# Inverse roots of a decoder layer started by one reciprocal-root activation instead of a logarithm and an exponential

## The chip, the cores and the metric

The kernel runs on one core of a Trainium2 chip. The metric is the device time of one execution in microseconds (us), as the median of several runs.

## The reference

One inference step of one decoder layer, for 256 prompt tokens and 8 decode tokens (264 columns, `T`) that share the weights; the width is 2048.

```
x = x + 1/2 * SwiGLU_1(RMSNorm(x))
h = RMSNorm(x); h @ w_in -> retention q/k/v/gate, attention q/k/v, indexer q/k/weights, two branch gates
A = retention(q, k, v), RMS-normed per head, * silu(gate)
B = top-k sparse attention, q and k RMS-normed per head
x = x + (sigmoid(g_A) * (A @ w_ret_out) + sigmoid(g_B) * (B @ w_att_out)) @ w_o
x = x + 1/2 * SwiGLU_2(RMSNorm(x))

def rms_norm(x, g):
    y = x * lax.rsqrt(mean(x * x, -1) + EPS)
    return y * g
```

Every RMS norm needs the inverse square root of a mean of squares.

## The kernel before

Activations lie transposed in SBUF: 128 features by 264 columns a block. Each weight block of 128 output features (`mblock`, L254 to L256 for its products) arrives in pieces of 128x1024 as 32-bit floats. ScalarE copies a piece to a rounded high part (`wh`, L248), VectorE or, for some pieces of the middle stage, GpSimd subtracts to get the low part (`wl`, L251), and TensorE adds up three products for each 128x128 block (high by high, high by low, low by high). Four buffers each of `wr`, `wh` and `wl` let the two splits run ahead, and three PSUM buffers (`ps`) let TensorE run up to three blocks ahead of whoever reads them.

The order of the work: the first FFN (weights `w1a`, `w2a`), then the middle stage (combined input projection, indexer, retention, attention, output projections), then the second FFN. In the middle stage the small tasks are generators in named queues; a weight block calls `step` with rates and so deals them out between weight products. A planner that estimates durations puts the instructions of each engine in order, with priorities (`ahead`), and in the middle stage only TensorE keeps the order of the program; ScalarE, VectorE, GpSimd and the DMA queues are ordered by the planner. At run time every engine works through its own list in order, so an instruction that waits holds up what stands behind it.

There are ten inverse roots, all by `root` (L262, L263) and `newton` (L266 to L268, VectorE). Three are for the norms of the model width (`Norm.done` through `rsqrt`, 128x264): at the start of the first FFN, of the middle stage and of the second FFN. Six go through `rms_roots` (128x528): two for the attention keys (`k_task`) and four for the retention heads (`group_norm`, which then scales `ro` at L1068). One is for the attention queries (`q_roots`, 128x33), whose result also scales rows that are written to DRAM and read back.

ScalarE evaluates a function only while a table that holds it is loaded; the program contains an ACT_TABLE_LOAD wherever the next function is not in the table loaded before. The other functions of ScalarE are Copy, Identity, Square, Relu, Silu (L325, L1192), Sigmoid (L1077) and the Exp of the two softmaxes (L768 for `psc` of the prompt, L858 for `sd` of decode).

Of the kernel before, what the change touches and what calls it, by code (L numbers as in the profile page):

```python
# [13 lines left out]
AF = mybir.ActivationFunctionType  # L14
# [108 lines left out]
def layer(ctx: ExitStack, tc: tile.TileContext, xT, gains, consts, dmat, didx, pt, state, cidx, ck, cv,  # L123
          w1a, w2a, wik, win, wro, wao, wo, w1b, w2b,
          yT, o_st, o_k, o_v, o_ik, o_sts):
    nc = tc.nc
# [26 lines left out]
    def wt(s="w", shape=(P, T), dt=F32, tag="w", bufs=8):  # L153
        return work.tile(list(shape), dt, tag=tag, name=nm(s), bufs=bufs)
# [104 lines left out]
        return ps[:m, :T]  # L259

    def root(ms, y, t):
        nc.scalar.activation(t, ms, AF.Ln)  # L262
        nc.scalar.activation(y, t, AF.Exp, scale=-0.5)  # L263

    def newton(y, ms, t):
        nc.vector.tensor_tensor(t, y, y, op=ALU.mult)  # L266
# [3 lines left out]
    def rsqrt(src, y, ms, t):  # L270

        nc.vector.tensor_scalar(ms, src, EPS, None, op0=ALU.add)
        root(ms, y, t)
        newton(y, ms, t)
# [393 lines left out]
    def rms_roots(sums):  # L668

        ss, y, t = (mt(n, (P, 2, T)) for n in ("ss", "y", "t"))  # L670
        for j, f in enumerate(sums):
            pq = aux()
            f(pq[:, :T])
            nc.scalar.activation(ss[:, j, :], pq[:, :T], AF.Identity, bias=epst)
        yield
        root(ss, y, t)
        yield
        newton(y, ss, t)
        yield y
# [468 lines left out]
    def q_roots():  # L1148
        qsq = mt("qsq", (P, NB, AH))
        nc.scalar.activation(qsq.rearrange("p b h -> p h b"), QS, AF.Square)  # L1150
        nc.vector.tensor_scalar(QS, QS, gqs, None, op0=ALU.mult)
        qrow = mt("qrow", (P, NB, AH))
        nc.vector.tensor_copy(qrow.rearrange("p b h -> p h b"), QS)
        yield
        pq = aux()
        nc.tensor.matmul(pq[:, :1], qsq.rearrange("p b h -> p (b h)"), ones128[:, :1], start=True, stop=True)
        pr = auxm()
        nc.tensor.transpose(pr[:, :P], qrow.rearrange("p b h -> p (b h)"), ident)
        qm, qt = st([P, 33], tag="qm", bufs=1), st([P, 33], tag="qt", bufs=1)
        qy = st([P, 33], tag="qy", bufs=1)  # L1160
        nc.vector.tensor_scalar(qm[:, 32:], pq[:, :1], EPS, None, op0=ALU.add)
        nc.vector.tensor_scalar(qm[:, :32], QSS.rearrange("p h t -> p (h t)"), EPS, None, op0=ALU.add)
        root(qm, qy, qt)
        newton(qy, qm, qt)
        nc.vector.tensor_copy(qsr, qy[:, 32:])
        nc.vector.tensor_copy(QR.rearrange("p h t -> p (h t)"), qy[:, :32])
        rt = mt("rt", (P, P))
        nc.scalar.activation(rt, pr[:, :P], AF.Copy, scale=qsr)
        nc.scalar.dma_start(rows[2], rt)
        yield  # L1170
# [46 lines left out]
    for m in range(KB):  # L1217
        ps = mblock(wao[m], 16, AHI, ALO)
        t = wt("at")
# [101 lines left out]
```

## Time and profile before

| | |
|---|---|
| median of 3 runs (lowest to highest) | 2666.53 us (2664.01 to 2667.66) |
| profiled execution, its own time | 2688.78 us |
| its span, first to last instruction | 2686.8 us |
| TensorE matmuls busy | 2614.1 us, 97% of the span |
| VectorE busy | 1534.2 us, 57% |
| ScalarE busy | 1172.4 us, 44% |
| GpSimd busy | 703.3 us, 26% |
| mean granted TensorE clock | 0.987 of full |

The times of single instructions below come from the profiled execution. It took 22 us more than the median of the runs, so a sum made of its rows is a difference to its own time and is carried to the median as a difference. In the rows PE is TensorE, DVE VectorE, ACT ScalarE, POOL GpSimd, SP the engine that issues DMAs; a q behind a name is the engine's instruction queue; xN merges N neighbouring instructions.

### The profile page before, as it was taken

What the parts mean: (1) busy time and instruction counts of PE and PEld (TensorE: products, weight loads), DVE (VectorE), ACT (ScalarE), POOL (GpSimd) and SP (SyncE); (2) the same over time, 40 slices, a digit from 0 to 9 for tenths busy, and PEclk for the clock granted to TensorE, in tenths of its full rate; (3) what the DMA queues carried; (4) which work ended last, traced back from release to release, by engine and by line L of the source; (5) the groups of instructions that cost most, each with busy time, mean ns of one, the idle gap of its engine ahead of it and who ended that gap; (6) DMA issues with size and microseconds to landing.
All of it is one profiled execution on the core that took longest, in us unless ns stands there. A gap on an engine that the chain in (4) does not pass through costs nothing.

```text
span 2686.8 us, 51545 instructions
## 1 busy us (share of the span) xinstructions
PE 2614.1 (97%) x21207; PEld 2586.1 (96%) x21207; DVE 1534.2 (57%) x2288; ACT 1172.4 (44%) x1559; POOL 703.3 (26%) x575
## 2 busy tenths in 40 slices
PE   7999999999999999999988899999999999999999
PEld 7999999999998899989888899999999999999999
DVE  6555555555564777534689745556655555554554
ACT  5443344334453434533546644444544334433443
POOL 3110011001265353245388353231111001100110
PEclk9999999999999999999999999999999999999999
DMA  6556555665575455456686566666577666765655
GB/s 217 181 181 181 181 182 181 183 183 183 170 240 181 138 179 171 128 181 218 219 290 219 182 202 226 207 217 201 182 238 231 210 189 224 240 207 181 216 165 174
DMA packets 173965, 529.09 MB, mean 197 GB/s; under 512 B 22705, under 2 KB 43761, under 8 KB 173729
## 3 DMA queue, kind: packets, MB, share of 16 engines
q1 hardware_dynamic: 148384, 488.31, 57.5%
q10 hardware_dynamic: 19440, 21.90, 2.4%
q0 software_dynamic: 5904, 15.59, 1.7%
q8 instruction: 166, 2.72, 0.4%
q14 instruction: 71, 0.57, 0.1%
HBM read 504.12 MB, written 21.60 MB: 196 GB/s over the span
## 4 chain that ended last, share of the span: by engine, by line
PE 87%; issue 3%; POOL 3%; DVE 2%; ACT 2%; DMA 2%; ACTq 0%; SPq 0%; POOLq 0%; DVEq 0%
PE ps L254 28%; PE ps L255 28%; PE ps L256 28%; POOL sb L958 1%; POOL wl L251 1%; POOL pr L836 1%; ACT wh L248 1%; DVE ro L1068 0%; DVE wl L251 0%; DVE psc L775 0%; DMA gs<-s 0%; DMA x<-xT 0%; PE aux L1038 0%; DMA qb<-rows 0%; DMA qq<-rows 0%
## 5 line engine op out<-in xcount | busy, mean ns | idle before, releaser
L248 ACT ACTIVATE wh<-wr 128x1024 fp32r<-128x1024 f32 x866 | 901.1, 1043 | 1339.3 <-PE ps L255 882.8
L251 DVE TENSOR_TENSOR wl<-wr,wh 128x1024 fp32r<-128x1024 f32 (+2 forms) x798 | 983.4, 1233 | 674.4 <-ACT wh L248 636.0
L254 PE MATMUL ps<-hi,wh 128*128 128x264 f32 x4624 | 1335.1, 289 | 20.3 <-ACT hi L287 10.2
L256 PE MATMUL ps<-hi,wl 128*128 128x264 f32 x4624 | 1321.6, 286 | 10.7 <-DVE wl L251 5.5
L255 PE MATMUL ps<-lo,wh 128*128 128x264 f32 x4624 | 1322.6, 286 | 5.1 <-issue 3.7
L254 PEld LDWEIGHTS ps<-hi,wh 128*128 128x128 f32 x4624 | 879.8, 190 | 29.6 <-issue 11.7
L256 PEld LDWEIGHTS ps<-hi,wl 128*128 128x128 f32 x4624 | 877.2, 190 | 14.6 <-DVE wl L251 7.0
L255 PEld LDWEIGHTS ps<-lo,wh 128*128 128x128 f32 x4624 | 879.2, 190 | 8.0 <-issue 5.3
L255 PE MATMUL ps<-hl,wh 128*128 128x264 f32 x1408 | 399.1, 284 | 0.4 <-issue 0.4
L256 PE MATMUL ps<-hh,wl 128*128 128x264 f32 x1408 | 398.9, 283 | 0.0
L254 PE MATMUL ps<-hh,wh 128*128 128x264 f32 x1408 | 398.8, 283 | 0.0
L327 POOL TENSOR_TENSOR s<-s,rstd 128x264 f32<-128x264 f32 x88 | 116.5, 1324 | 1012.1 <-ACT s L325 1012.1
L256 PEld LDWEIGHTS ps<-hh,wl 128*128 128x128 f32 x1408 | 264.4, 188 | 0.5 <-issue 0.5
L255 PEld LDWEIGHTS ps<-hl,wh 128*128 128x128 f32 x1408 | 264.7, 188 | 0.0
L254 PEld LDWEIGHTS ps<-hh,wh 128*128 128x128 f32 x1408 | 264.6, 188 | 0.0
L251 POOL TENSOR_TENSOR wl<-wr,wh 128x512 fp32r<-128x512 f32 x136 | 180.8, 1351 | 254.0 <-ACT wh L248 226.5
L836 POOL TENSOR_TENSOR pr<-qb,kb 128x512 f32<-128x512 f32 x64 | 102.3, 1629 | 22.4 <-issue 8.8
L988 POOL TENSOR_TENSOR kv<-ku,rvs 128x512 f32<-128x512 f32 x32 | 33.6, 1050 | 217.7 <-DMA ku<-rows 205.1
L990 DVE SCALAR_TENSOR_TENSOR su<-su,kv 128x256 f32<-128x256 f32 x64 | 24.4, 422 | 95.6 <-POOL kv L988 95.6
L359 POOL DMA_INDIRECT kt<-cidx,kix x64 | 72.8, 1138 | 18.1 <-issue 17.5
L334 DVE TENSOR_TENSOR h<-ps,s 128x264 f32<-128x264 f32 x88 | 38.1, 433 | 65.5 <-PE ps L256 61.5
L255 PE MATMUL ps<-alo,wh 128*128 128x264 f32 x256 | 72.9, 285 | 0.0
(317 smaller groups left out, 2310.8 us busy)
## 6 DMA issues: line engine op xcount, KB each, us to landing
wr<-win SPq DMA_DIRECT2D x224, 512.0 KB
wr<-w1a SPq DMA_DIRECT2D x176, 512.0 KB
wr<-w1b SPq DMA_DIRECT2D x176, 512.0 KB
wr<-w2a SPq DMA_DIRECT2D x80, 512.0 KB
wr<-w2b SPq DMA_DIRECT2D x80, 512.0 KB
wr<-wro SPq DMA_DIRECT2D x32, 512.0 KB
wr<-wao SPq DMA_DIRECT2D x32, 512.0 KB
wr<-wo SPq DMA_DIRECT2D x32, 512.0 KB
```

The source lines that it names most:

```text
L248: nc.scalar.activation(wh[:, :n, :m], wr[:, :n, :m], AF.Copy)
L251: eng.tensor_sub(wl[:, a:e, :m], wr[:, a:e, :m], wh[:, a:e, :m])
L254: nc.tensor.matmul(ps[:m, :T], wh[:, k, :m], hi[g], start=g == 0, stop=False)
L255: nc.tensor.matmul(ps[:m, :T], wh[:, k, :m], lo[g], start=False, stop=False)
L256: nc.tensor.matmul(ps[:m, :T], wl[:, k, :m], hi[g], start=False, stop=g == nk - 1)
L327: nc.gpsimd.tensor_mul(s2, s, rstd)
L334: nc.vector.tensor_mul(h, pu, s2)
L359: nc.gpsimd.indirect_dma_start(out=KT[p][pg // 8][:, o:o + PG], out_offset=None, in_=cidx, in_offset=bass.IndirectOffsetOnAxis(ap=kix[:, p ...
L836: nc.gpsimd.tensor_mul(pr[:, a:a + 1], qb[:, a:a + 1], k[:, a:a + 1].to_broadcast([P, 1, 4, P]))
L958: nc.gpsimd.tensor_mul(sb[:, a:a + 2], sb[:, a:a + 2], qq[:, a:a + 2, None, :].to_broadcast([P, 2, 2, P]))
L988: nc.gpsimd.tensor_mul(kv, k[:, :, None, :].to_broadcast([P, 2, 2, P]), v.to_broadcast([P, 2, 2, P]))
L990: nc.vector.scalar_tensor_tensor(s[:, i], s[:, i], g1[h + i], kv[:, i], op0=ALU.mult, op1=ALU.add)
```

## The change

The logarithm and the exponential of minus one half of it are replaced by one activation that gives the reciprocal of the root of the absolute value. The intermediate tile `t` is no longer written by ScalarE; it is still used by the Newton step, which stays.

```
     def root(ms, y, t):
-        nc.scalar.activation(t, ms, AF.Ln)
-        nc.scalar.activation(y, t, AF.Exp, scale=-0.5)
+        nc.scalar.activation(y, ms, AF.Abs_reciprocal_sqrt)
```

## Rows read from the trace of the kernel before

**Rows 1.** The page, busy time of each engine.

```profile
PE 2614.1 (97%) x21207; PEld 2586.1 (96%) x21207; DVE 1534.2 (57%) x2288; ACT 1172.4 (44%) x1559; POOL 703.3 (26%) x575
```

**Rows 2.** Windows by stage: stretch, its length, busy time (count) of each engine, PEclk, DMA.

```profile
40.00:796.00 756.00, 754.16 (x6226) 753.80 (x6225) 402.90 (x466) 318.58 (x390) 111.43 (x91) 1.00 0.61 186
...
1420.00:1540.00 120.00, 105.35 (x795) 101.28 (x793) 101.64 (x141) 80.69 (x139) 67.83 (x50) 0.96 0.60 195
...
1940.00:2680.00 740.00, 740.00 (x6096) 740.00 (x6095) 394.81 (x497) 298.29 (x344) 84.29 (x74) 1.00 0.66 208
```

**Rows 3.** Groups by line, ScalarE: shapes, count | busy us, mean ns | idle before.

```profile
L262 ACT ACT_TABLE_LOAD x10 | 12.8, 1283 | 0.3
L263 ACT ACT_TABLE_LOAD x10 | 12.8, 1283 | 0.2
...
L262 ACT ACTIVATE t<-ss 128x528 f32<-128x528 f32 x6 | 3.9, 646 | 0.1
...
L262 ACT ACTIVATE qt<-qm 128x33 f32<-128x33 f32 x1 | 0.2, 233 | 0.0
```

**Rows 4.** Timeline of ScalarE, first root: start, us, instruction [idle before <-what ended it].

```profile
36.71 0.42 ACT L262 ACTIVATE t<-ms 128x264 f32<-128x264 f32 x1
37.16 1.28 ACT L263 ACT_TABLE_LOAD   x1
38.45 0.42 ACT L263 ACTIVATE rstd<-t 128x264 f32<-128x264 f32 x1
```

**Rows 5.** Timeline of TensorE, the first wait behind that root.

```profile
44.44 0.36 PE L254 MATMUL ps<-hi,wh 128*128 128x264 f32 x1 [1.47 <-DVE h L334]
```

**Rows 6.** Timelines of VectorE and TensorE, first key root.

```profile
1112.35 0.71 DVE L266 TENSOR_TENSOR t<-y 128x528 f32<-128x528 f32 x1 [3.31 <-ACT y L263]
...
1113.72 0.15 DVE L589 TENSOR_SCALAR fill<-aux 128x1 f32<-128x1 f32 x1
```

```profile
1113.92 0.70 PE L1033 MATMUL aux<-rs,vr 128*128 128x256 f32 x2 [1.52 <-DVE fill L589]
```

**Rows 7.** Windows of low granted clock, columns as in rows 2.

```profile
1114.50:1121.30 6.80, 6.21 (x25) 5.54 (x24) 2.96 (x5) 0.77 (x2) 2.11 (x2) 0.50 0.39 117
...
1541.20:1548.00 6.80, 5.63 (x26) 5.63 (x27) 4.24 (x11) 4.62 (x8) 5.58 (x5) 0.50 0.83 298
```

**Rows 8.** Chain of waits behind the query root: start, us, what.

```profile
1293.55 1.84 DMA rows<-rt
...
1296.31 7.65 DMA qq<-rows
```

**Rows 9.** Timelines of VectorE and TensorE behind that read.

```profile
1306.67 1.22 DVE L953 TENSOR_REDUCE rd<-sb 128x8 f32<-128x1024 f32 x1 [3.93 <-POOL sb L958]
```

```profile
1319.22 0.51 PE L254 MATMUL ps<-hi,wh 128*128 128x264 f32 x1 [2.51 <-ACT wh L248]
1322.90 0.59 PE L256 MATMUL ps<-hi,wl 128*128 128x264 f32 x1 [2.96 <-DVE wl L251]
```

**Rows 10.** Timelines of ScalarE, VectorE and TensorE, second head root.

```profile
1469.87 1.28 ACT L1077 ACT_TABLE_LOAD   x1
```

```profile
1473.85 0.77 DVE L266 TENSOR_TENSOR t<-y 128x528 f32<-128x528 f32 x1 [1.41 <-ACT y L263]
```

```profile
1492.38 0.91 PE L1060 MATMUL aux<-sq,ones 128*128 128x264 f32 x3 [2.69 <-DVE psc L755]
```

**Rows 11.** Timeline of TensorE, third head root.

```profile
1514.27 0.49 PE L792 MATMUL aux<-pts,vn 128*128 128x128 f32 x2 [1.07 <-ACT pts L786]
```

**Rows 12.** Timelines of VectorE, ScalarE and TensorE, fourth head root.

```profile
1531.12 0.71 DVE L266 TENSOR_TENSOR t<-y 128x528 f32<-128x528 f32 x1 [5.07 <-ACT y L263]
```

```profile
1539.30 0.42 ACT L1192 ACTIVATE s<-g 128x264 f32<-128x264 f32 x1 [4.23 <-DVE g L1190]
1539.74 1.28 ACT L858 ACT_TABLE_LOAD   x1
```

```profile
1542.37 0.66 PE L869 MATMUL aux<-C,sd 128*128 128x128 f32 x2 [4.10 <-DVE sd L861]
```

## The prediction, written before the changed kernel had run

> **What bounds the kernel now.** I read the page first: matmuls fill 97% of the span and ScalarE, the engine that is changed, 44% [rows 1]. Work taken from ScalarE is worth nothing by itself; it counts only where TensorE stands still, or runs at its lower clock, because a root came late. The windows by stage say where that can be: between 40 and 796 us TensorE stands still for 1.8 us of 756, and between 1940 and 2680 us not at all, but between 1420 and 1540 us for 14.7 of 120 us, at a granted clock of 0.96 [rows 2]. So both FFNs are closed to a gain, except the first microseconds, and the middle stage is open. From there I went to the groups of ScalarE for the price of the edit [rows 3], then to the ten roots one by one in the timelines, asking of each which wait of TensorE ends behind it [rows 4 to 12].
>
> **What is removed.** Each of the ten roots is now a table load, a Ln, a second table load and an Exp: L262 and L263 have ten loads each of 1283 ns [rows 3]. Ln and Exp therefore do not share a loaded table here. The new root needs its table and one activation. I take 1283 ns for its load, since the loads of both functions cost that to the ns, and the Ln's own duration for its activation at each size (646, 425 and 233 ns; the middle one is the 0.42 us of rows 4): same tiles, same engine [rows 3, 4]. A price from zero up to that of the pair replaced would be the bounds; nothing that is added exceeds what is removed.
>
> How many loads go: one for each root, ten. Three more go between neighbours. Between the middle stage's norm and both key roots ScalarE runs only functions for which this trace shows no load (copies, squares, identities and relus), so the key roots find the table in place: two more loads. In the second head root a sigmoid with a load of its own stands between Ln and Exp [rows 10], so the table changes four times around it; with one activation it changes twice: one more besides the root's own. The count of the whole program should fall by 13. That is 13 x 1.283 = 16.7 us, and with the ten Exp of about 6 x 0.646 + 3 x 0.425 + 0.233 = 5.4 us ScalarE loses 22.1 us of its 1172.4.
>
> The Trainium skill, in "ScalarE: Activation LUTs", section "Table sets: the hidden batching unit", speaks against the change: it says that one set holds both Ln and Exp and that the pair costs one load. By that rule no load of a lone root would be saved, only the 0.42 to 0.65 us of one activation, and the sum below would shrink to about a third. This trace differs: a load stands ahead of each of the two, ten times, and so the rule gets no chance among the rivals. The same section says that the cheap functions are in every set; the absence of loads ahead of copies here agrees.
>
> **What of it lies on the path**, root by root in order of time. The shift of a root is the distance from the start of Ln to the start of Exp, since the one activation ends where Ln ended.
>
> First FFN: Ln begins at 36.71 and Exp at 38.45, so the root is 1.74 us earlier [rows 4]. TensorE waits 1.47 us for `h`, which waits for this root through the gate [rows 5]. The shift covers it: 1.47 us. Since TensorE then hardly stands still until 796 us, this is kept.
>
> The norm of the middle stage and that of the second FFN: TensorE does not wait behind either; the blocks in the three PSUM buffers hide the 1.7 us. If that cover were gone each would be worth up to 1.7 us. I take 0.
>
> First key root: VectorE stands 3.31 us for it, and behind the Newton step in VectorE's list waits `fill`, which frees the buffer that TensorE needs: TensorE waits 1.52 us [rows 6]. Without two loads and one activation the root ends 2 x 1.28 + 0.65 = 3.2 us earlier, more than the wait, so 1.5 us. Right behind the wait the granted clock is 0.50 (1.2 GHz) for 6.8 us [rows 7]: half of it, 3.4 us, is lost. Other waits of such a length, the 1.47 us above, show no such stretch behind them [rows 2, 5], so I do not know whether this one alone brought it. Between 0 and 3.4 us I take half, 1.7. The second key root has no wait of TensorE behind it: 0.
>
> Query root: its Newton step is followed by the write of `rows`, and on SP's queue the read of `qb` waits for that write; the reads of `sb` and `qq` for the retention stand behind it, and then weights [rows 8]. GpSimd and then VectorE wait for `qq` (3.93 us) [rows 9], and after them come the softmax of the first attention group and, late, the weight splits for which TensorE waits 2.51 and 2.96 us [rows 9]. The root comes a load and a small activation earlier, 1.28 + 0.23 = 1.5 us. Between 0 and 1.5 I take 1.5, since each link follows the one before without slack in the chain.
>
> Head roots. The first finds VectorE busy until its result is there: 0. At the second VectorE stands 1.41 us for it, and TensorE later 2.69 us for `psc` from the same list [rows 10]; between 0 and 2.69 I take the 1.41 that VectorE gets back. At the third TensorE waits 1.07 us for `pts`, which stands in ScalarE's list behind the softmax and both loads of the root [rows 11]; a shift of 1.9 us covers it: 1.07. At the fourth VectorE stands 5.07 us for the root and TensorE 4.10 us for the decode softmax `sd` [rows 12]. But the exponential of `sd` stands in ScalarE's list behind a Silu that needs the end of a weight block [rows 12], so in the order of now only some 0.4 us are won; were the planner to put the exponential first, all 4.10, and the 3.4 us that the low clock behind it costs [rows 7]. I take 0.4.
>
> Sum: 1.47 + 1.5 + 1.7 + 1.5 + 1.41 + 1.07 + 0.4 = 9.1 us. The profiled execution would take 2688.8 - 9.1 = 2679.7 us. It lies 22 us above the median of the runs, so I carry the difference: 2666.5 - 9.1 = 2657.4 us, 0.34% less. The upper bound of the gain takes every term at its end: 1.47 + 1.5 + 3.4 + 1.5 + 2.69 + 1.07 + 4.1 + 3.4 = 19.1 us, and with the two hidden norms 22.5: 2644 us. The lower bound is the first term alone, 1.5 us: 2665.0.
>
> A second rule of that page, section "What ACT_TABLE_LOAD costs", gives 2.66 us for a switch of set, a drain of 1.38 us included. By it the 13 loads would be worth an estimated 34.6 us of ScalarE. The rows do not agree: the second load starts 0.03 us after the Ln ends, and the Exp 1.29 us after that load's start, with no room for a drain [rows 4].
>
> **Rivals.** *No measurable change.* The middle stage has many chains with almost no slack beside one another, and the planner will order ScalarE and VectorE anew, since its estimates change too. Where TensorE stops waiting for a root it may wait as long for GpSimd's or VectorE's next task. For it: between 1420 and 1540 us VectorE is busy 101.6 of 120 us and so near a bound itself [rows 2]. Against it: several of the waits end directly on a root. It would leave the first term and little more: about 2663 us, within 0.2%.
>
> *Slower, by one mechanism:* the planner puts a burst of softmax exponentials ahead of a weight split on ScalarE. The prompt's exponentials come eight to a group, and one such burst already cost TensorE 2.51 + 2.96 us [rows 9]; with a stretch of low clock like those of rows 7, of which 3.4 us are lost, that is 8.9 us. One more such event pays back the whole sum; it decides for slower once the middle terms (7.6 us) are also replaced by waits on that burst, 1.47 gained against 8.9 lost: about 2674 us. For it: an earlier root lets such a burst start earlier. Against it: less work on ScalarE makes weight splits earlier too.
>
> *The change does not do what it says:* the new table would lack the copy, and the ten copies after the roots would each need a load again. That returns ten of 13 loads and leaves 1 to 4 us of gain, about 2664 us. All tables in this trace serve copies without a load, so I hold it for unlikely.
>
> **How the numbers follow.** Forecast (faster, around 2657 us): 0.61. No change by the first rival 0.23, by the last 0.02. Slower 0.14. I take 0.2%, 5.3 us, as what a measurement can tell from no change. The range goes from 2645, near the upper bound of the gain, to 2668 us, which takes in the no-change cases and leaves out most of the slower one. For the forecast alone the range is 2645 to 2661.
>
> **What would show it.** Right: 30 table loads in place of 43, none at all ahead of the key roots; ScalarE near 1150 us busy; the waits of 1.47, 1.52 and 1.07 us gone; the roots' activations at 0.65, 0.43 and 0.23 us. Wrong: the same number of loads; the new activation longer than the Ln; the sum of TensorE's waits in the middle stage unchanged although VectorE no longer waits for a root; or a low clock in new places. A gain over 15 us would mean that the decode exponential moved ahead of the Silu, or that a clock term which I halved or left out came in whole.

## The result, and the profile after

The changed kernel takes 2652.51 us (median of 5, 2651.47 to 2656.55) against 2666.53 us (median of 5, 2663.67 to 2668.71): a ratio of 0.9949, 95% interval 0.9938 to 0.9960, 14.0 us less. The forecast was 2657.4 us, 9.1 us less, in a range of 2645 to 2668.

The page after, span and busy time:

```profile
span 2649.5 us, 51519 instructions
...
PE 2596.8 (98%) x21207; PEld 2574.0 (97%) x21207; DVE 1524.5 (58%) x2288; ACT 1152.2 (43%) x1536; POOL 707.9 (27%) x575
```

ScalarE lost 20.2 us against [rows 1] (22.1 were forecast); TensorE's count is the same. The groups of ScalarE after, all lines that hold a table load, and the new root at its sizes:

```profile
L1076 ACT ACT_TABLE_LOAD x11 | 14.1, 1283 | 0.2
...
L262 ACT ACT_TABLE_LOAD x8 | 10.3, 1283 | 0.2
L767 ACT ACT_TABLE_LOAD x5 | 6.4, 1283 | 0.5 <-ACT s L1076 0.4
...
L262 ACT ACTIVATE y<-ss 128x528 f32<-128x528 f32 x6 | 3.9, 646 | 0.6 <-DMA o_st<-so 0.5
...
L324 ACT ACT_TABLE_LOAD x2 | 2.6, 1283 | 1.4 <-DVE g L322 1.4
L1191 ACT ACT_TABLE_LOAD x2 | 2.6, 1283 | 0.0
L181 ACT ACT_TABLE_LOAD x1 | 1.3, 1283 | 1.2 <-PEq L1304 1.2
L857 ACT ACT_TABLE_LOAD x1 | 1.3, 1283 | 0.0
```

11 + 8 + 5 + 2 + 2 + 1 + 1 = 30 loads, where there were 43. There are eight for ten roots, so two roots found their table in place, and the new activation takes 646 ns, as the Ln did [rows 3]. The lines above 261 have moved up by one.

The span fell by 37.3 us, far more than the time. Some 20 us of that are not the change's: in the first profile TensorE stood several times with nothing that it waited for ("issue" is idle time for which the profile shows no wait). The waits of TensorE by cause, kernel before, first profile: us in total, times, longest.

```profile
PE ps L254 <- issue: 5.0, 7, 1.5
...
PE ps L255 <- issue: 4.1, 7, 0.9
```

and one of the two places where these stand, 825.7 to 838.5 us, in windows of the kernel before, first the first profile, then the second (the run `again`):

```profile
825.70:838.50 12.80, 6.23 (x25) 4.63 (x26) 3.09 (x5) 1.36 (x2) 9.22 (x9) 0.72 0.34 105
```

```profile
825.70:838.50 12.80, 12.80 (x108) 12.80 (x106) 6.84 (x7) 4.24 (x4) 10.06 (x10) 1.00 0.72 239
```

In the second, TensorE is busy throughout at the full clock, and the span is 2667.2 us. Against that profile the change is worth 17.7 us of span.

The planner had a small part in it: the order of TensorE, GpSimd and the DMA queue of SP is the same instruction by instruction in both kernels, and on VectorE ten instructions and on ScalarE a few changed places. Two of these moves stand at roots that count. Behind the fourth head root the copy to `sd` now comes after the four `ro` products. At the first key root `fill`, which stood between the instructions of the Newton step [rows 6], now stands ahead of them; timeline of VectorE after:

```profile
1097.56 0.16 DVE L588 TENSOR_SCALAR fill<-aux 128x1 f32<-128x1 f32 x1 [2.41 <-PE aux L548]
...
1099.27 1.07 DVE L265 TENSOR_TENSOR t<-y 128x528 f32<-128x528 f32 x1 [0.85 <-PE aux L1033]
```

### The profile page after: what moved, and what is told of

Its sections match the earlier page's. It is cut to its first block, busy times and chain, and to the rows that moved or that the text cites. A ratio compares the mean times of both kernels' runs of the same rounds, so it can differ in the third digit from the quotient of the medians.

```text
span 2649.5 us, 51519 instructions
## 1 busy us (share of the span) xinstructions
PE 2596.8 (98%) x21207; PEld 2574.0 (97%) x21207; DVE 1524.5 (58%) x2288; ACT 1152.2 (43%) x1536; POOL 707.9 (27%) x575
## 4 chain that ended last, share of the span: by engine, by line
PE 88%; POOL 3%; DVE 3%; issue 3%; DMA 2%; ACT 1%; ACTq 0%; SPq 0%; POOLq 0%; DVEq 0%
PE ps L254 29%; PE ps L255 29%; PE ps L256 28%; POOL pr L835 2%; POOL sb L957 1%; POOL wl L251 1%; DVE wl L251 1%; ACT wh L248 1%; DMA qb<-rows 0%; DMA gs<-s 0%; DVE sTs L826 0%; DMA x<-xT 0%; DVE ro L1067 0%; DVE psc L774 0%; PE aux L1032 0%
```

## Experiments

**The kernel before, profiled again** (`again`), no edit.

> The kernel before, unchanged, profiled a second time. If the TensorE waits that end on nothing in the first profile (825 to 838 us and 1148 to 1155 us, with low clock behind them, about 20 us in all) belong to that one execution, they are absent here and the span is near 2665 us, while the waits behind roots (1.47, 1.52, 2.69, 1.07 and 4.10 us) come back at the same places. If they belong to the kernel, and the change removed them, they are here again and the span is near 2687 us.

2669.2 us, span 2667.2 us. The waits that end on nothing are absent, those behind roots are back. Timeline of TensorE, first key root, second and fourth head root:

```profile
1100.74 1.22 PE L1033 MATMUL aux<-rs,vr 128*128 128x256 f32 x2 [1.93 <-DVE fill L589]
...
1473.65 1.13 PE L1060 MATMUL aux<-sq,ones 128*128 128x264 f32 x4 [2.31 <-DVE psc L755]
...
1523.63 0.41 PE L869 MATMUL aux<-C,sd 128*128 128x128 f32 x2 [4.10 <-DVE sd L861]
```

The low clock behind them is shorter than in the first profile. Windows at granted clock 0.50 behind the first and the last of these waits:

```profile
1100.80:1104.20 3.40, 3.36 (x9) 2.62 (x9) 3.37 (x5) 0.38 (x1) 2.62 (x2) 0.50 0.00 0
1524.00:1527.40 3.40, 3.40 (x17) 3.40 (x17) 3.31 (x8) 3.08 (x5) 2.79 (x3) 0.50 0.73 253
```

3.4 us each, so 1.7 us lost at each place, where [rows 7] had twice that.

**The change split in three.** Each root gets a switch, and three kernels set it for the key roots (`keys`), for the fourth head root (`last`), and for the seven others (`rest`).

```
     def root(ms, y, t, new=False):
+        if new:
+            nc.scalar.activation(y, ms, AF.Abs_reciprocal_sqrt)
+            return
         nc.scalar.activation(t, ms, AF.Ln)
         nc.scalar.activation(y, t, AF.Exp, scale=-0.5)
...
-        for y in rms_roots([total(0), total(1)]):     # norm_heads
+        for y in rms_roots([total(0), total(1)], True):     # keys
-            for y in rms_roots([total(0), total(1)]):     # group_norm
+            for y in rms_roots([total(0), total(1)], hq == 3):     # last; hq < 3 in rest
```

> The new activation in the two key roots alone, Ln and Exp in the other eight. By the reading of the profile after, the wait of 1.52 us and the 0.6 us next to it go, and with them the whole 6.8 us of low clock behind: 2.1 + 3.4 = 5.5 us less than before. By the prediction half of the low clock goes: 3.2 us. If the gain went with the ScalarE work removed (5 of the 22 us), it would be 3 us. TensorE's later waits stay.

2665.57 us (12 runs) against 2669.70 (25 runs), ratio 0.9986, 0.9977 to 0.9994: 3.7 us less, between 1.6 and 6.1. Windows, the stretch of the first key root:

```profile
1094.00:1106.00 12.00, 12.00 (x95) 11.74 (x94) 7.90 (x16) 5.87 (x10) 2.99 (x2) 1.00 0.35 112
```

TensorE is busy for all 12 us at the full clock. Wait and low clock went together; between the sizes of the expectation, 3.2, 5.5 and 3, the interval does not decide. `fill` stands ahead of the Newton step here too, so this run does not tell the earlier root from the changed order; `copy`, below, does.

> The new activation in the fourth head root alone. By the reading of the profile after, the decode softmax is ready in time, the wait of 4.10 us and the 6.8 us of low clock behind it go: 7.5 us less than before. By the prediction a Silu that needs the end of a weight block holds the softmax, so 0.4 us. If the gain went with the ScalarE work removed (1.9 of the 22 us), it would be 1.2 us.

2664.51 us (12 runs), ratio 0.9982, 0.9973 to 0.9991: 4.8 us less, between 2.4 and 7.2. That excludes both 0.4 and 1.2. With the low clock as the second profile has it, 4.1 + 1.7 = 5.8 us fit better than 7.5. Windows, from the last instructions of the root to behind the decode softmax:

```profile
1513.00:1528.00 15.00, 15.00 (x135) 14.66 (x135) 9.49 (x22) 11.35 (x15) 9.56 (x8) 1.00 0.61 194
```

> The new activation in the other seven roots: three norms, query root, first three head roots. The first wait of 1.47 us goes. By the profile after, the second head root gives 1.4 us of its wait and 1.7 us of low clock, the third gives nothing, and the query root gives nothing, because a read of a stored gate in ScalarE's queue holds the scaled rows until it has landed: 4.6 us less in all. By the prediction 1.47 + 1.5 + 1.41 + 1.07 = 5.5 us. If the gain went with the ScalarE work removed (15 of the 22 us), it would be 9.5 us.

2662.73 us (8 runs), ratio 0.9976, 0.9964 to 0.9988: 6.4 us less, between 3.2 and 9.6. The three parts add up to 3.7 + 4.8 + 6.4 = 14.9 us, the whole gave 14.0; each of the parts is uncertain by 2 to 3 us. Shares of ScalarE's work would be 3, 1.2 and 9.5; the middle one is outside its interval.

**Loads against activations** (`copy`, `load`). One keeps the number of activations and drops the loads, the other the reverse (its extra Ln writes one column that is overwritten).

```
-        nc.scalar.activation(y, ms, AF.Abs_reciprocal_sqrt)
+        nc.scalar.activation(t, ms, AF.Abs_reciprocal_sqrt)     # copy
+        nc.scalar.activation(y, t, AF.Copy)
...
+        nc.scalar.activation(y[c], ms[c], AF.Ln)     # load: c is one column
         nc.scalar.activation(y, ms, AF.Abs_reciprocal_sqrt)
```

> As after the change, but each reciprocal root writes the intermediate tile and a copy of the same size follows, so that the loads are gone and the number of full activations is that of before. If the gain is the loads', about 13 of the 14 us stay (the first wait keeps 0.2 us, the others are covered by the load alone): 0.995 of before. If the Exp itself made the gain, little stays: 0.999 to 1.

> As after the change, but a Ln of one column stands ahead of each reciprocal root (its result is overwritten), so that the number of table loads is that of before while the second full activation is gone. If the gain is the loads', 2 to 4 us remain of it: about 0.999 of before. If the second activation made the gain, 0.995 to 0.997.

`copy` has 30 loads and 2671.66 us (7 runs), ratio 0.9960, 0.9942 to 0.9979. `load` has 43 and 2687.83 us (11 runs), ratio 1.0009, 0.9999 to 1.0019. So the gain is the loads': with them back none of it is left, not even the 2 to 4 us that I expected there (the short Ln takes 0.2 us, ten times). Nor is it the planner's: `copy` has VectorE's instructions in the order of the kernel before, all 2288, and keeps the gain; `load` has them in an order like that after the change, `fill` ahead of the Newton step included, and loses it. In `load` TensorE waits for the decode softmax almost as long as before, in `copy` less than half of it (first fence `load`, second `copy`, timelines of TensorE):

```profile
1537.05 0.66 PE L870 MATMUL aux<-C,sd 128*128 128x128 f32 x2 [3.79 <-DVE sd L862]
```

```profile
1519.99 0.41 PE L869 MATMUL aux<-C,sd 128*128 128x128 f32 x2 [1.58 <-DVE sd L861]
```

This group, and the one after it, ran on another chip than the split; here the kernel before took 2686.14 us (30 runs). All four profiles of the group have waits of TensorE that end on nothing, 9.2 us in `copy`, 15.0 in `load`, 18.8 in `tanh` and 18.5 in `sgpool`, so single times of this group say less than those of the split.

**Fewer loads still** (`tanh`, `tanh2`). The gates' sigmoid becomes a tangent; 0.5 (1 + tanh(x/2)) is the same function.

```
-        nc.scalar.activation(s, g, AF.Sigmoid)
+        nc.scalar.activation(s, g, AF.Tanh, scale=0.5)
...
-        nc.vector.tensor_mul(MG[m], ps, sgate(0, m))
+        nc.vector.scalar_tensor_tensor(MG[m], sgate(0, m), 1.0, ps, op0=ALU.add, op1=ALU.mult)
...
-        split(t2, MHI[m], MLO[m])
+        nc.scalar.activation(MHI[m], t2, AF.Copy, scale=0.5)
+        nc.vector.scalar_tensor_tensor(MLO[m], t2, 0.5, MHI[m], op0=ALU.mult, op1=ALU.subtract)
```

> As after the change, and the sigmoids of the gates become a hyperbolic tangent of half the argument (one added and the product halved in instructions that were there), so that gates and softmax share a table and some 14 more loads, 18 us of ScalarE, go in the stretch where TensorE waits most. If loads cost time wherever ScalarE is in a queue of work, 4 to 8 us less than after: 0.992 to 0.9935 of before. If they count only where an instruction that TensorE waits for stands right behind, as the prediction had it, the wait of 2.5 us for a weight split goes and little else: 0.994.

> The tangent in place of the sigmoids, again. Its first profile has 18 us less ScalarE work than after and the same sum of waits that end on an instruction (38 against 39 us). If loads off the path are free, the time of after within 3 us. If they cost anywhere, 4 to 8 us less than after.

**The gate reads off ScalarE's queue** (`sgpool`, `sgpool2`), **and both** (`tanhsg`):

```
-        nc.scalar.dma_start(t, gs[which, i])
+        nc.gpsimd.dma_start(t, gs[which, i])
```

> As after the change, but the reads of the stored gates are issued from GpSimd's queue, where they hold up nothing at the query root. If the read in ScalarE's queue is what took the query root's gain, the scaled rows go out 1.5 us or more earlier, the read of qq and GpSimd's first product follow, and the wait of 2.51 us for a weight split shrinks: 1.5 to 5 us less than after. If the rows were not on the path, the time is that of after, 0.995 of before.

> The reads of the stored gates on GpSimd's queue, again. In its first profile the waits of TensorE that end on an instruction, with low clock behind them, come to about 49 us against 56 us after the change; if that holds against after on one chip, 3 to 8 us less than after. If the first comparison (0.996 of before) tells the truth, the time of after.

> Both: the tangent and the gate reads on GpSimd's queue. If the two act on different waits, the sum of what each gave against after: 3 to 8 us less. If the softmax burst ahead of the weight splits at the first attention group is bound by VectorE once ScalarE is free, no better than the gate reads alone.

**The changed kernel once more** (`after2`), in the group of the last four:

> The changed kernel, unchanged, beside the three others of this group, because the group before it ran on a chip where TensorE's waits that end on nothing (around 820 and 1150 us) came in nearly every execution, in sizes from 9 to 35 us with their low clock. 0.995 of before again if the gain does not hang on them; its table loads and waits behind roots are those of the first profile after.

Measured (us, median; the kernel before stood at 2686.14 in the group of `tanh` and `sgpool`, the one of `copy` and `load`, and at 2680.89, of 24 runs, in that of the last four):

| run | time | runs | ratio to before | 95% interval |
|---|---|---|---|---|
| tanh | 2680.64 | 11 | 0.9978 | 0.9965 to 0.9990 |
| sgpool | 2678.13 | 12 | 0.9959 | 0.9941 to 0.9977 |
| after2 | 2672.68 | 12 | 0.9970 | 0.9953 to 0.9988 |
| tanh2 | 2670.69 | 12 | 0.9962 | 0.9943 to 0.9981 |
| sgpool2 | 2668.57 | 7 | 0.9949 | 0.9930 to 0.9968 |
| tanhsg | 2662.27 | 6 | 0.9927 | 0.9906 to 0.9949 |

`after2` is 8.2 us faster than before, between 3.2 and 12.6, an interval that overlaps the first one. `tanh2` took ten loads from it (20 are left), not the 14 that I expected, since the sigmoids next to roots keep theirs; its time is within the interval of `after2`. The groups of ScalarE in `tanh2`, where no line of the softmax of the prompt has a load any more:

```profile
L262 ACT ACT_TABLE_LOAD x8 | 10.3, 1283 | 0.2
L1076 ACT ACT_TABLE_LOAD x6 | 7.7, 1283 | 0.1
```

The Trainium skill, "ScalarE: Activation LUTs", section "Table sets: the hidden batching unit", says that Exp and the tangent are in one set; these groups agree.

So 12.8 us of loads in this stretch bought nothing that can be told. The medians differ by 2.0 us and the intervals allow some us more, so that the smaller gain of the expectation, 4 us, is not excluded; 12.8 us is. `sgpool2` alone cannot be told from `after2` either; its reads raise GpSimd's busy time from 706.7 to 722.7 us and VectorE's from 1529.2 to 1545.6. Both together can: the interval of `tanhsg` lies below that of `after2`, and it is the fastest kernel here, 18.6 us below the kernel before. Why the two act together was not tested by a run of its own, but the profiles show where to look. Timelines of TensorE at the weight splits behind the query root, `after2`, `sgpool2`, `tanhsg`:

```profile
1299.47 0.59 PE L256 MATMUL ps<-hi,wl 128*128 128x264 f32 x1 [3.06 <-DVE wl L251]
...
1308.39 0.39 PE L254 MATMUL ps<-hi,wh 128*128 128x264 f32 x1 [0.41 <-ACT wh L248]
...
1312.07 0.47 PE L256 MATMUL ps<-hi,wl 128*128 128x264 f32 x1 [3.17 <-DVE wl L251]
```

```profile
1302.91 0.59 PE L256 MATMUL ps<-hi,wl 128*128 128x264 f32 x1 [3.17 <-DVE wl L251]
```

```profile
1305.77 0.39 PE L256 MATMUL ps<-hi,wl 128*128 128x264 f32 x1 [1.67 <-DVE wl L251]
```

All waits there from 0.25 us on add up to 5.8 and 6.5 us in the two profiles before, 7.3 and 6.6 after, 6.4 and 7.3 in `tanh` and `tanh2`, but 3.5, 3.2 and 1.7 in `sgpool`, `sgpool2` and `tanhsg`. So in these profiles the gate reads hold up TensorE here by some 3 us. In `tanh2` the wait for `wh` is gone, as expected, but the last one for `wl` has grown from 3.17 to 4.88 us, so VectorE set the time there.

## Why the prediction was right, point by point

**Direction, loads, path.** The step from [rows 1] to the loads, and from there to what TensorE waits for behind each root, held. 13 loads went, none stands ahead of the key roots, and `copy` and `load` show that the loads make the gain. TensorE's waits that end on an instruction add up to 58.1 and 60.9 us in the two profiles before, to 49.4 and 49.8 us in the two after, and to 47.8 us in `copy`: after the change 8 to 12 us less, where the sum of the prediction has 7.4 us of waits and 1.7 of low clock. That a load saved elsewhere is worth nothing fits `tanh2`, within the few us that its interval leaves open.

That the sum came out near is in part luck. Two terms of it, 2.6 us together, were not there, and one was too small by 4.4 us.

**First FFN, 1.47 us.** Held: ScalarE's timeline after has the root end at 36.97 us, 1.9 us before the first profile's, and the wait of [rows 5] has gone.

```profile
35.25 1.28 ACT L262 ACT_TABLE_LOAD   x1
36.55 0.42 ACT L262 ACTIVATE rstd<-ms 128x264 f32<-128x264 f32 x1
```

**Key root, 1.5 + 1.7 us.** Held in size: 3.7 us measured for it alone. The mechanism is only in part the one predicted: in the kernel after, `fill` no longer waits for the root at all, since it stands ahead of the Newton step. `copy`, with the old order and without the loads, and `load`, with the new order and all loads, both lack the wait, so either would have been enough; the earlier root was a sufficient reason, as the prediction said, but not the only one. To halve the low clock was a choice between 0 and 3.4 us, and that the second profile has 1.7 us there is luck.

**Query root, 1.5 us.** Failed: the step "each link follows the one before without slack in the chain" left out ScalarE's own queue. Timelines of ScalarE, first before the change, then after it, then `sgpool2` (`gs` is the stored gate, `sg` its read):

```profile
1289.08 0.33 ACTq L1078 DMA_DIRECT2D gs<-s  x1
1290.37 0.23 ACT L262 ACTIVATE qt<-qm 128x33 f32<-128x33 f32 x1
...
1292.78 0.33 ACTq L1205 DMA_DIRECT2D sg<-gs  x1
...
1293.55 0.33 ACTq L1169 DMA_DIRECT2D rows<-rt  x1
```

```profile
1260.66 0.33 ACTq L1077 DMA_DIRECT2D gs<-s  x1
1261.94 0.23 ACT L262 ACTIVATE qy<-qm 128x33 f32<-128x33 f32 x1
...
1264.31 0.36 ACTq L1204 DMA_DIRECT2D sg<-gs  x1
1264.71 0.37 ACT L1167 ACTIVATE rt<-auxm,qsr 128x128 f32<-128x128 f32 x1 [1.59 <-DVE wl L251]
1265.11 0.33 ACTq L1168 DMA_DIRECT2D rows<-rt  x1
```

```profile
1269.90 0.23 ACT L262 ACTIVATE qy<-qm 128x33 f32<-128x33 f32 x1
1271.38 0.35 ACT L1167 ACTIVATE rt<-auxm,qsr 128x128 f32<-128x128 f32 x1
1271.76 0.33 ACTq L1168 DMA_DIRECT2D rows<-rt  x1
```

Between the root and the scaled rows stands the issue of a read of a gate just written, and it waits for that write to land: it comes 3.7 us behind the issue of the write before the change and 3.7 us after it, whatever the root does. The profile lists the idle time under another name. From the start of the first activation to the issue of the rows' write it is 1265.11 - 1261.94 = 3.2 us after the change and 1293.55 - 1290.37 = 3.2 us before: the time saved went into this wait whole. With the reads in another queue it is 1.9 us, and TensorE's waits at the weight splits behind it are some 3 us shorter in the profiles (above); as a time of its own `sgpool2` does not show it. A single one of these waits says little: that for `wh` [rows 9] is 2.51 us after the change, but 0.41 us in `after2`, the same kernel.

**Second head root, 1.41 us.** Held: the wait of 2.69 us in the first profile and 2.31 us in the second is now 1.27 us (1.16 in `after2`).

```profile
1462.50 1.13 PE L1059 MATMUL aux<-sq,ones 128*128 128x264 f32 x4 [1.27 <-DVE psc L754]
```

**Third head root, 1.07 us.** Failed. Timeline of ScalarE, then of TensorE, after:

```profile
1465.78 0.65 ACT L262 ACTIVATE y<-ss 128x528 f32<-128x528 f32 x1
1466.44 1.28 ACT L1076 ACT_TABLE_LOAD   x1
1469.34 0.43 ACT L1076 ACTIVATE s<-g 128x264 f32<-128x264 f32 x1 [1.61 <-DVE g L1074]
```

```profile
1483.74 0.49 PE L791 MATMUL aux<-pts,vn 128*128 128x128 f32 x2 [1.29 <-ACT pts L785]
```

ScalarE, earlier by some 1.9 us, now stands 1.61 us for the input of the next sigmoid, which VectorE makes when its own list comes to it. The wait for `pts` is 1.29 us where it was 1.07 (1.00 in `after2`, 1.33 in `again`): here VectorE set the time, as the first rival said for the whole stretch.

**Fourth head root, 0.4 us.** This is the term that was mis-sized: 4.8 us, between 2.4 and 7.2. The step that failed is that a Silu "needs the end of a weight block" and so holds the decode softmax whatever the root does. It is true that the Silu stands ahead, after the change too. But its input waited in VectorE's list, behind the Newton step and the four `ro` products, and so behind the root. Timelines of ScalarE (the Exp of before, the one activation of `last`) and of VectorE, first profile before, then `last`:

```profile
1530.45 0.64 ACT L263 ACTIVATE y<-t 128x528 f32<-128x528 f32 x1
```

```profile
1510.00 0.65 ACT L263 ACTIVATE y<-ss 128x528 f32<-128x528 f32 x1
```

```profile
1533.57 3.77 DVE L1068 SCALAR_TENSOR_TENSOR ro<-ro,G,y 128x264 f32<-128x264 f32 x4
...
1538.85 0.41 DVE L1190 TENSOR_TENSOR g<-ps,rstd 128x264 f32<-128x264 f32 x1
```

```profile
1510.68 0.71 DVE L269 TENSOR_TENSOR t<-y 128x528 f32<-128x528 f32 x1 [1.11 <-ACT y L263]
...
1512.90 1.70 DVE L1071 SCALAR_TENSOR_TENSOR ro<-ro,G,y 128x264 f32<-128x264 f32 x4
...
1516.63 0.42 DVE L1193 TENSOR_TENSOR g<-ps,rstd 128x264 f32<-128x264 f32 x1
```

Most of the gain is the root itself. Before, a sigmoid with a load of its own stood between Ln and Exp here too, as at the second head root, so that the Exp began 3.97 us after the Ln (1530.45 - 1526.48); now the root ends where the Ln ended. VectorE's wait for it fell from 5.07 us [rows 12] to 1.11. A smaller part lies behind it: the four products took 3.77 us while two of GpSimd's subtractions ran (1533.85 to 1536.64), and take 1.70 us now that those come at 1517.08. The Silu's input was there 5.95 us after VectorE had taken up the root (1516.63 - 1510.68) in place of 7.73 (1538.85 - 1531.12), but then the Silu waits for its own table load, so that from the start of the root's first load to the softmax's Exp it is 4.5 us less in all (1520.05 - 1508.70 = 11.35, before 1541.04 - 1525.19 = 15.85). That is more than the 4.10 us which TensorE had waited, and the softmax was in time. `copy`, with VectorE's old order, has 1.58 us of this wait left, so the moved copy to `sd` is not what took the greater part. The row names no weight block [rows 12]: the Silu waits for `g` of VectorE, and I had read the block into it.

**Rivals.** The softmax burst did not get worse by anything like the 8.9 us of the second rival: the waits at the weight splits behind it add up to 5.8 and 6.5 us before and 7.3 and 6.6 after. The planner, on which it and the first rival leaned, kept its order but for the few moves named above. That the new table lacks the copies is excluded by the count of loads.

## What to carry to other kernels

Price a table load by the instruction that stands behind it in line, not by its duration: here 13 loads gave 14 us (8 in a second comparison), and ten more, in the stretch where TensorE waits most, gave nothing that could be told. When a stall goes, read the list of every engine between the cause and the one that counts, its DMA issues too, because an issue that waits for a landing takes a gain as fully as an instruction does. A difference of two profiles needs a second profile of the same kernel beside it: some 20 of 37 us were one execution's. And compare the order of each engine's instructions before a gain is laid to a shorter one: at the first key root the planner had moved the waiting instruction as well.

## What the runs showed of the hardware

TensorE stood around 815 to 840 us, around 1130 to 1165 us or at both places with nothing to wait for that the profile shows, and then ran at a granted clock of 0.50, 1.2 GHz (831.2 to 841.5 us in the first profile). That was so in the first profile of the kernel before, in neither `again` nor the first profile after nor the three kernels of the split, and in all eight profiles of the two later groups, which ran on another chip than the split. One window of such a place after the change (`after2`) is

```profile
1131.00:1150.00 19.00, 12.27 (x68) 10.74 (x67) 3.35 (x4) 5.51 (x7) 8.69 (x9) 0.73 0.27 83
```

TensorE is busy for 12.3 of 19 us at a clock of 0.73. The kernel before has medians of 2666.5 and 2669.7 us in the first comparison and the split, and of 2686.1 and 2680.9 us in the two later groups; that these waits make the difference is not shown. What causes them was not tried and stays open.

The same wait is followed by low clock of different length in two executions of one program: 6.8 us in the first profile, 3.4 us in the second, behind the first key root and again behind the fourth head root.
